# Reordering the opening's up blocks and computing more up blocks of the second feed-forward by seven products

## The chip, the cores and the metric

The kernel runs on one core of a Trainium2 chip, as one launch. The metric is the device time of one execution in microseconds (us). One core has five engines with instruction streams of their own: TensorE (PE in the profile; its weight loads are PEld), VectorE (DVE), ScalarE (ACT), GpSimd (POOL) and SyncE (SP), which issues most transfers. An engine runs its instructions in their order and waits for the others by semaphores. Sixteen DMA engines move data between HBM and the on-chip buffer. TensorE writes its sums into eight banks of PSUM, each 128 x 512 numbers of four bytes.

## The reference, cut to what matters

One layer with a context and a latent sequence of 256 tokens each and a model width of 2048. Each half-step feed-forward has 5632 hidden channels.

```python
def adaln(x, g, mod, i):
    return rms_norm(x, g) * (1 + mod[:, i + 1, None, :]) + mod[:, i, None, :]

def half_step_ffn(x, mod, i, g, w_up, w_down):
    h = adaln(x, g, mod, i)
    a, b = jnp.split(h @ w_up, 2, axis=-1)
    return x + 0.5 * mod[:, i + 2, None, :] * ((jax.nn.silu(a) * b) @ w_down)

mod_l = (silu(c) @ w_mod + b_mod).reshape(B, 9, D_MODEL)        # mod_c likewise from c_ctx
xl = half_step_ffn(xl, mod_l, 0, g_norm[0], w_ffn1_up, w_ffn1_down)
xc = half_step_ffn(xc, mod_c, 0, g_norm[0], w_ffn1_up, w_ffn1_down)
...                                                             # token mixing of both sequences
xl = half_step_ffn(xl, mod_l, 6, g_norm[2], w_ffn2_up, w_ffn2_down)
return rms_norm(xl, g_final)
```

So the first feed-forward works on 512 tokens, the second on the 256 latent ones alone.

## The kernel before, in words

**Numbers in two parts.** Every matrix operand of 32 bits is held as a high part (rounded to the format that TensorE multiplies) and a low part (the rest). `split` (line 110) makes both from a raw weight tile of 128 x 2048, in two halves of 128 x 1024: ScalarE copies the high part (line 118), VectorE subtracts it (line 119). `hi` and `lo` have four buffers each, `raw` three. `mm3` (line 138) makes one product from three matmuls: high x high (140), high x low and low x high (141 and 142). `load_split` (line 131) loads a tile on SP's queue and splits it, and takes one step of whatever is in `beside["load"]`.

**The hidden channels** come in 44 columns of 128; four columns make a block, so there are eleven blocks (0 to 10). A column f has an a and a b half, each of which sums 16 rows of weights k = 0 to 15 (2048 inputs).

**The opening** (lines 459 to 612). The scale and shift of the first feed-forward's norm aren't known at the start: they come from 32 units of 1 MB of modulation weights. The loop over `BLOCKS` (line 577: row blocks 0, 1, 2-4, 4-6 ... 14-16) loads a row block's units, sums them on TensorE (`mod_sums`, line 541; output `tr<-mraw,cP`), and, for one unit of each two-row block, on VectorE against the conditions `cB`. It turns the sums, scales the transposed x into the operands `hhi` and `hlo` for these rows, and then adds these rows' products to the columns f = 0, 1, 2 (`products`, line 413), which hold all six `mm` banks of PSUM until the end. The columns of one row block run between the sums of the next. Ahead of the loop stands the preparation: x and ctx are loaded, `spread` (line 483) lays the two condition vectors over all partitions by matmuls against ones (`mm<-raw,ones`), first the context's, then the latents'; `x_tile` squares, sums and scales each of four x tiles; `x_turned` transposes row 0. Instructions of this stage are pinned to the program's order (most carry line 78).

After the loop, `tail` (line 664) takes silu(a) x b of columns 0 to 2, and column f = 3 is computed by itself from four more tiles (lines 680 to 688).

**Seven products.** Blocks 1 to 10 of the first feed-forward's up part (`quad`, line 761) cut tokens and inputs in two each, and combine seven products of half size instead of eight; the operands for that (`n1`, `s2`, `s4`, `s3`) are sums and differences of token quarters that `token_forms` (line 698) makes on VectorE and ScalarE ahead of and during the first such block. The weight combinations arise in two chain buffers by accumulating transfers on POOL's queue (`accum`, issued at line 652).

**The second feed-forward** (from line 1780). Blocks 1, 3, 5, 7 and 9 are computed by seven products (`quad`, line 1920: 7 products x 2 tiles, 12 matmuls a tile), blocks 2, 4, 6, 8 and 10 plainly (`up`, line 2000: 8 tiles, 24 matmuls a tile). A `down` (line 2034) multiplies a finished hidden block by four tiles of the down weights, 24 matmuls each, and adds the sums into `acc2`. `units` strings up and down tiles together; after each unit the loop at the end of the stage takes tiles of the seven-product blocks at `PACE2` = 70/73 per unit, so the two kinds alternate nearly one to one. `turned` transposes a finished hidden tile. In a seven-product block of this stage (the list `order`) the two chain buffers receive three pairs of accumulating loads and the two `ra` tiles one pair; `plain`, `loaded` and `again` are plain loads. `mod_late` adds one modulation sum on VectorE (line 211, `sraw`) in some of the loads, paced by ((32, 62),). Then come `down` of block 9 and `last2`, the last block with the final norm.

Of the kernel before, what the change touches and what calls it, by code (L numbers as in the profile page):

```python
# [19 lines left out]
P = 128  # L20
D = 2048
# [12 lines left out]
PACE2 = 70 / 73  # L34

BLOCKS = ((0, 1), (1, 2)) + tuple((k, k + 2) for k in range(2, 16, 2))
# [13 lines left out]
def tile_layer(ctx: ExitStack, tc: tile.TileContext, I: dict, out: bass.AP):  # L50
# [59 lines left out]
    def split(raw, n=2048):  # L110

        half = n // 2
        parts = []
        for h in range(2):
            hi = wp.tile([P, 1024], F32R, tag="hi", name="hi", bufs=4)[:, :half]
            lo = wp.tile([P, 1024], F32R, tag="lo", name="lo", bufs=4)[:, :half]
            src = raw[:, h * half : (h + 1) * half]
            nc.scalar.activation(hi, src, AF.Copy)  # L118
            vector[0].tensor_tensor(lo, src, hi.bitcast(F32), op=ALU.subtract)  # L119
# [339 lines left out]
    pre = [[bank(), bank()] for _ in range(NPRE)]  # L459
    with pool(name="st", bufs=1) as st:  # L460
        scratch.append(st)
        cP = st.tile([P, KT, 32], F32, name="cP")
# [20 lines left out]
        def spread(s, m):  # L483
            for q in range(4):
                b = pre[q // 2][q % 2]
                w = slice(q * CB, (q + 1) * CB)
                tensor[0].matmul(b, ones[:32, :], m[:, w], start=True, stop=True)
                if s:
                    nc.scalar.activation(cB[:, s, w], b, AF.Copy)
                else:  # L490
                    vector[0].tensor_copy(cB[:, s, w], b)

        def x_tile(s, t, shared=False):
# [3 lines left out]
            for cb in range(NCB):  # L497
                if not (shared and cb % 2):
# [5 lines left out]
            for c in (slice(0, 256), slice(256, D)):  # L504
                vector[0].tensor_scalar(x[:, c], x[:, c], r, None, op0=ALU.mult)

# [12 lines left out]
        tc.keep_in_program_order(nc.sync.dma_start(vecs, I["vecs"]))  # L519
        diagonals = [diagonal(s) for s in (CTX, LAT)]  # L520
        spread(CTX, diagonals[0])
        x_tile(CTX, 0)
        x_turned(0, CTX, 0)
        spread(LAT, diagonals[1])
        for s, t in ((CTX, 1), (LAT, 0), (LAT, 1)):
            x_tile(s, t, s == LAT and t == 1)
            x_turned(0, s, t)
# [7 lines left out]

        def mod_unit():
            raw = st.tile([P, 2048], F32, tag="mraw", name="mraw", bufs=4)
# [38 lines left out]
        turns = []  # L576
        for k0, k1 in BLOCKS:
            kk = slice(k0, k1)
            following = products(I["w_up1"], pre, k0, k1, hhi, hlo, k0 == 0)
            if k1 - k0 == 2:  # L580
                raw = mod_unit()
            for i in range(2):
                for _ in mod_sums(i, k0 if i else k1 - 1, k1, following if i else iter(())):
                    steps(prods, 3 - (k1 - k0))
                if k0 == 0:
                    mod_turned()
# [6 lines left out]
            mod_turned()  # L593
            steps(prods)
            for s in (CTX, LAT):
                scale_of(0, s, kk)
            if k1 - k0 == 1:
# [5 lines left out]
                x_scaled(k0, tb)  # L603
            else:
# [6 lines left out]
        drain(prods)  # L611
        vector[0], tensor[0] = nc.vector, nc.tensor
# [40 lines left out]
    with pool(name="f1u", bufs=1) as f1u:  # L653
# [10 lines left out]
        def tail(f, pab):  # L664
            sa = ca_tile()
            nc.scalar.activation(sa, pab[0], AF.Silu)
            nc.vector.tensor_tensor(sa, sa, pab[1], op=ALU.mult)
            nc.sync.dma_start(hidd[0][:, :, f, :], sa.rearrange("p (t c) -> p t c", t=4))

# [8 lines left out]
        for f in range(NPRE):  # L678
            tail(f, pre[f])
        for f in range(NPRE, FB):  # L680
            pab = []
            for ab in range(2):
                wt = load_split(I["w_up1"][f, ab])
                b = bank()
                for k in range(KT):
                    mm3(b, *wt(slice(k * P, (k + 1) * P)), hhi[:, k, :], hlo[:, k, :], k == 0, k == KT - 1)
                pab.append(b)
            tail(f, pab)
# [68 lines left out]

        def c12_tile():
            return f1u.tile([P, CB], F32, tag="c12", name="c12", bufs=2)
# [89 lines left out]
        def first_steps(step):  # L849
            if step in (1, 2, 3, 4, 5, 6):  # L850
# [21 lines left out]
        raws, place0 = [], []  # L872
        quad(1, first_steps)
# [900 lines left out]
    with f2x:  # L1774
# [53 lines left out]
        beside["load"] = mod_late(f8cm.__enter__(), 8, 9, ((32, 62),))  # L1828
# [3 lines left out]
        QUADS = range(1, LAST, 2)  # L1832
# [16 lines left out]
        def token_forms():  # L1849
# [20 lines left out]
            v = ra_tile()[:, :1024].rearrange("p (k c) -> p k c", k=8)  # L1870
# [9 lines left out]
            v = ra_tile()[:, :1024].rearrange("p (k c) -> p k c", k=8)  # L1880
            difference(v, a11, a21)
            put(s3, v)
# [3 lines left out]
        turn = []  # L1886
        summed = set()

        def turned():

            if not turn:
                return
            n, t, sa, sign = turn[0]
# [19 lines left out]
        def wait_turn(n, t, sa, sign):  # L1913
            turn.append((n, t, sa, sign))
# [5 lines left out]
        def quad(n):  # L1920
# [41 lines left out]
            def again(q):  # L1962
                if n + 2 in QUADS:
                    nc.sync.dma_start(chain_[q], part(n + 2, 0, q))

            def loaded(q):
                ra[q] = ra_tile()
                nc.sync.dma_start(ra[q], part(n, 1, 2 + q))
                return ra[q]

            def plain(q):
# [262 lines left out]
```

## Time and profile before

| what | value |
|---|---|
| median of 3 runs | 2656.78 us (2656.41 to 2657.49) |
| the profiled execution | 2654.22 us, its span 2652.5 us |
| granted TensorE clock, mean | 0.998 |
| bytes read from HBM / written | 659.87 MB / 17.89 MB |
| plain transfers (q1) / POOL's (q0) | 500.07 MB / 177.22 MB |
| modulation units of the opening | 32 of 1024 KB, 7.5 us from issue to landing in the median |

In a table of windows each row is a stretch of the span: its ends and length, the busy time and number of instructions of each engine, the granted clock, the mean busy share of the DMA engines and their GB/s. In a timeline a row has a start, a duration, the engine, the line, the instruction, output <- inputs, the shapes and the count; in brackets how long the engine was idle before it and what released it. In a table of groups the last numbers are the busy time, the mean duration in ns, and the idle time of the engine before them. Line 78 is the helper that pins the opening's order.

### The profile page before, as it was taken

How to read it: one execution, taken by the hardware profiler on the slowest of the kernel's cores; microseconds unless marked ns; L12 is line 12 of the kernel's file. 1: busy time of each engine (PE TensorE's matmuls, PEld its weight loads, DVE VectorE, ACT ScalarE, POOL GpSimd, SP SyncE). 2: the span in 40 equal slices, each digit the busy share in tenths (PEclk: the TensorE clock that was granted, in tenths of full speed). 3: DMA queues.
4: the chain of work that ended last, by engine and by line, in shares of the span. 5: the costliest groups of instructions: out<-in, count | busy, mean ns of one | idle time of the engine just before them, and what ended most of it. 6: DMA issues, size and time to landing. Idle time of an engine off the chain costs nothing. (4 is left out here: it accounts for less than half of the span.)

```text
span 2652.5 us, 33763 instructions
## 1 busy us (share of the span) xinstructions
PE 2603.8 (98%) x12718; PEld 2153.9 (81%) x12718; DVE 2132.9 (80%) x2918; ACT 1349.5 (51%) x1682; POOL 208.3 (8%) x259
## 2 busy tenths in 40 slices
PE   8999999999999999999999999999999999999998
PEld 4688887888888878888889888877898888888887
DVE  5697888878888788888886979797698777777877
ACT  4354444554444555444455336355476655555554
POOL 0000001000001100010110000111000000000001
PEclk9999999999999999999999999999999999999999
DMA  9979999999999988889986867574479998989975
GB/s 360 340 214 270 264 278 262 263 276 281 261 283 263 274 233 239 223 208 229 231 243 224 308 232 242 199 270 167 167 262 291 288 291 291 288 275 283 276 231 175
DMA packets 135028, 679.98 MB, mean 256 GB/s; under 512 B 14152, under 2 KB 23624, under 8 KB 73552
## 3 DMA queue, kind: packets, MB, share of 16 engines
q1 hardware_dynamic: 107216, 500.07, 50.8%
q0 software_dynamic: 27360, 177.22, 34.2%
q8 instruction: 100, 1.64, 0.2%
q10 hardware_dynamic: 288, 0.52, 0.1%
q14 instruction: 64, 0.52, 0.1%
HBM read 659.87 MB, written 17.89 MB: 256 GB/s over the span
## 5 line engine op out<-in xcount | busy, mean ns | idle before, releaser
L118 ACT ACTIVATE hi<-raw 128x1024 fp32r<-128x1024 f32 (+3 forms) x542 | 560.8, 1039 | 639.1 <-PE mm L142 481.8
L119 DVE TENSOR_TENSOR lo<-raw,hi 128x1024 fp32r<-128x1024 f32 (+1 forms) x524 | 631.1, 1211 | 272.2 <-ACT hi L118 254.9
L118 ACT ACTIVATE hi<-chain 128x1024 fp32r<-128x1024 f32 x320 | 337.9, 1059 | 257.6 <-PE mm L142 135.7
L119 DVE TENSOR_TENSOR lo<-chain,hi 128x1024 fp32r<-128x1024 f32 x320 | 387.5, 1221 | 95.8 <-ACT hi L118 93.1
L140 PE MATMUL mm<-hi,hhi 128*128 128x512 f32 (+3 forms) x1024 | 390.7, 384 | 7.3 <-DVE c L755 6.8
L141 PE MATMUL mm<-lo,hhi 128*128 128x512 f32 (+3 forms) x1024 | 387.6, 379 | 0.2
L142 PE MATMUL mm<-hi,hlo 128*128 128x512 f32 (+3 forms) x1024 | 387.0, 378 | 0.0
L211 DVE SCALAR_TENSOR_TENSOR junk<-sraw,cBh 128x1024 fp8e5<-128x1024 f32 x192 | 234.4, 1221 | 24.8 <-DMA sraw<-in_w_mt 22.5
L140 PEld LDWEIGHTS mm<-hi,hhi 128*128 128x128 f32 x1024 | 192.3, 188 | 40.0 <-ACT hi L118 6.4
L142 PEld LDWEIGHTS mm<-hi,hlo 128*128 128x128 f32 x1024 | 192.5, 188 | 33.6
L141 PEld LDWEIGHTS mm<-lo,hhi 128*128 128x128 f32 x1024 | 192.7, 188 | 32.0 <-DVE lo L119 1.3
L142 PE MATMUL mm<-hi,hid2l 128*128 128x512 f32 x352 | 137.4, 390 | 0.0
L140 PE MATMUL mm<-hi,hid2h 128*128 128x512 f32 x352 | 137.2, 390 | 0.0
L141 PE MATMUL mm<-lo,hid2h 128*128 128x512 f32 x352 | 137.1, 389 | 0.0
L140 PE MATMUL mm<-hi,h2hi 128*128 128x512 f32 x320 | 125.0, 391 | 1.5 <-DVE sab L1813 1.5
L141 PE MATMUL mm<-lo,h2hi 128*128 128x512 f32 x320 | 124.6, 389 | 0.0
L142 PE MATMUL mm<-hi,h2lo 128*128 128x512 f32 x320 | 124.6, 389 | 0.0
L652 POOL DMA_DIRECT2D chain<-in_w_up1b x60 | 53.1, 886 | 739.4 <-DVE lo L119 654.4
L142 PE MATMUL mm<-hhi,lo 128*128 128x512 f32 (+1 forms) x288 | 100.4, 349 | 4.5 <-DVE lo L119 4.4
L140 PE MATMUL mm<-hhi,hi 128*128 128x512 f32 (+1 forms) x288 | 101.3, 352 | 0.0
L141 PE MATMUL mm<-hlo,hi 128*128 128x512 f32 (+1 forms) x288 | 99.4, 345 | 0.0
L211 DVE SCALAR_TENSOR_TENSOR sr<-sr,cBl 128x1024 f32<-128x1024 f32 x72 | 87.1, 1216 | 7.0 <-DMA sr<-in_w_mt 6.8
(479 smaller groups left out, 5483.8 us busy)
## 6 DMA issues: line engine op xcount, KB each, us to landing
raw<-in_w_dn SPq DMA_DIRECT2D x70, 1024.0 KB, 7.3
sraw<-in_w_mt SPq DMA_DIRECT2D x128, 512.0 KB, 7.5
chain<-in_w_up1b POOLq DMA_DIRECT2D x60, 1024.0 KB, 11.1
raw<-in_w_up2b SPq DMA_DIRECT2D x50, 1024.0 KB, 7.0
raw<-in_w_up1b SPq DMA_DIRECT2D x40, 1024.0 KB, 8.5
sr<-in_w_mt SPq DMA_DIRECT2D x69, 512.0 KB, 5.3
mraw<-in_w_m SPq DMA_DIRECT2D x32, 1024.0 KB, 7.5
chain<-in_w_dn POOLq DMA_DIRECT2D x30, 1024.0 KB, 8.8
```

Of the source, the lines that this page charges most:

```text
L118: nc.scalar.activation(hi, src, AF.Copy)
L119: vector[0].tensor_tensor(lo, src, hi.bitcast(F32), op=ALU.subtract)
L140: tensor[0].matmul(out_ap, sh, mh, start=first, stop=False, skip_group_check=skip)
L141: tensor[0].matmul(out_ap, sh, ml, start=False, stop=False, skip_group_check=skip)
L142: tensor[0].matmul(out_ap, sl, mh, start=False, stop=last, skip_group_check=skip)
L211: ins = nc.vector.scalar_tensor_tensor(junk() if junk else raw, raw, 1.0, cB[s], op0=ALU.mult, op1=ALU.mult, accum_out=mT[:, i, s, kt, h : ...
L652: accum = lambda dst, src: nc.gpsimd.dma_start(dst, src, accum_op=ALU.add)
```

## The change

In the opening, the three columns that a row block serves take turns: 0, 1, 2 for rows 0 to 4, then 1, 2, 3 to row 10, then 2, 3, 0. What a column lacks is done later: f = 3's rows 0 to 4 from the row block that begins at 6, f = 0's rows 4 to 10 from the one that begins at 12 (`LATER`), f = 1's rows 10 to 16 inside the first seven-product block (`back`). When column 0 or 1 gives up its two banks, its sums so far go to HBM (`put_by`) and are added back later by an accumulating load (`whole_sums`). The products of a load run in three passes over all its columns: the weights' high parts with the high parts of the activations, then with their low parts, then the weights' low parts. The preparation is woven: only the context's half of the spread stands first, the latents' four matmuls follow one by one, two of them behind the modulation sums of row 0; only 256 of the 2048 columns of each x tile are scaled at once, the rest during row blocks 0 and 2; the sums of squares are shared between ScalarE and VectorE.

The buffers of `split` become one ring of four slots for `hi` and one for `lo`. In the second feed-forward a whole tile is split at once (`split_whole`, two slots), and its products are ordered so that all that need the high part come first. The plain blocks are 2, 6 and 9; the other seven are computed by seven products. One accumulating pair of each such block becomes a plain load, made earlier, with an addition on VectorE (`added`). The token forms use `acc2` as scratch. The order of the tiles is a table (`places`), and `turned` waits until three tiles' worth of work has been issued since the tile was ready. The pace of `mod_late` is ((32, 52),).

```diff
-PACE2 = 70 / 73
+COLUMN_PLAN = _column_plan()     # fs = (0, 1, 2) if k1 <= 4 else (1, 2, 3) if k1 <= 10 else (2, 3, 0)
+PUT_BY = {(0, 4): 3, (1, 10): 0}
+LATER = {6: [(3, 0, 4)], 12: [(0, 4, 8), (0, 8, 10)]}
...
+    def split_whole(raw):
+        hi, lo = ring(2)
+        nc.scalar.activation(hi, raw, AF.Copy)
+        nc.vector.tensor_tensor(lo, raw, hi.bitcast(F32), op=ALU.subtract)
+        return lambda w: (hi[:, w], lo[:, w])
+    def high_first(*parts):
+        for out_ap, sh, sl, mh, ml, first, last in parts:
+            nc.tensor.matmul(out_ap, sh, mh, start=first, stop=False, skip_group_check=True)
+            nc.tensor.matmul(out_ap, sl, mh, start=False, stop=False, skip_group_check=True)
+    def low_last(*parts):
+        for out_ap, sh, sl, mh, ml, first, last in parts:
+            nc.tensor.matmul(out_ap, sh, ml, start=False, stop=last, skip_group_check=True)
...
+                for wl, tl in ((0, 0), (0, 1), (1, 0)):
+                    for o, (f, ab, k) in enumerate(each):
...
+                        tensor[0].matmul(slot[f][ab], wt(slice(o * P, o * P + P))[wl], (hhi, hlo)[tl][:, k, :], start=first, stop=bool(last))
...
+                        if done % (3 if g[0][2] - g[0][1] == 1 else 6) == 0:
+                            yield
...
+                            nc.scalar.activation(t, slot[f][ab], AF.Copy)
+                            nc.gpsimd.dma_start(put_by[f][ab], t)
...
+        def opening(following):
...
+            for n, (s, t) in enumerate(xs0):
+                scaled = x_sums(s, t, 2 if n else 3)
+                wide[n](vector[0].tensor_copy)
+                scaled(slice(0, 256))
+                rest.append(lambda scaled=scaled: scaled(slice(256, D)))
+                if n == 3:
+                    drain(mod_sums(0, 0, 1))
+                x_turned(0, s, t)
+                for q in {1: (0,), 2: (1,)}.get(n, ()):
+                    late(q)
+            mod_turned()
+            drain(mod_sums(1, 0, 1))
+            steps(following)
+            mod_turned()
+            for q in (2, 3):
+                late(q)
...
+            if k0 in LATER:
+                back = columns([[x] for x in LATER[k0]])
+                steps(back)
...
         def first_steps(step):
+            if step == 0:
+                steps(back)
+            if step in (1, 2, 3):
+                steps(back, 2)
+            if step == 4:
+                drain(back)
+                tail(0, *first_of[0], first_of[0][0])
+                first_of[1] = whole_sums(1)
+            if step == 7:
+                tail(1, *first_of[1], first_of[1][0])
...
+        back = columns([[(1, 10, 14)], [(1, 14, 16)]])
         quad(1, first_steps)
...
-        QUADS = range(1, LAST, 2)
+        PLAIN = (2, 6, 9)
+        QUADS = [n for n in range(1, LAST + 1) if n not in PLAIN]
...
+            def added(q):
+                nc.vector.tensor_tensor(chain_[q], chain_[q], ra[q], op=ALU.add)
...
-                (a12, plain, "Y", True, None, c11),
-                (n1, held, "Y", True, chained(1, 2), kept),
-                (s4, loaded, "Y", False, lambda q: accum(ra[q], part(n, 1, q)), p35),
+                (a12, plain, "Y", True, loaded, c11),
+                (n1, held, "Y", True, lambda q: added(0) if q else None, kept),
+                (s4, lambda q: ra[q], "Y", False, lambda q: (None if q else added(1), accum(ra[q], part(n, 1, q))), p35),
...
+            halves = iter((4, 0, 4, 0, 0, 4, 0, 0, 4, 0, 4, 0, 0, 4, 0))
...
+            for n in QUADS:
+                last = n == QUADS[-1]
+                for i in range(14):
+                    out.append(i in (range(3, 10) if last else (3, 4, 5, 6, 7, 9, 11, 13)) or n == QUADS[-2] and i == 8)
```

More of the change, by code (lines that the diff above doesn't have):

```diff
@@ L481, in diagonal, with spread, x_sums @@
             return m
[L483 to L493, printed above, removed]
+        def spread(s, m, q, b):
+            w = slice(q * CB, (q + 1) * CB)
+            tensor[0].matmul(b, ones[:32, :], m[:, w], start=True, stop=True)
+            return lambda copy: copy(cB[:, s, w], b)
+        def x_sums(s, t, n_act):
             x = xs0[s, t]
@@ L497, in x_tile @@
             for cb in range(NCB):
-                if not (shared and cb % 2):
+                if cb < n_act:
                     sumsq(ss4[:, cb : cb + 1], x[:, cb * CB : (cb + 1) * CB])
@@ L593, in tile_layer @@
             mod_turned()
+            while k0 == 2 and rest:
+                rest.pop(0)()
             steps(prods)
@@ L603, in tile_layer @@
                 x_scaled(k0, tb)
+                if not k0:
+                    rest.pop(0)()
+                    rest.pop(0)()
             else:
@@ L677, in tile_layer, with c12_tile @@
             first_chain(1, c)
[L678 to L688, printed above, removed]
+        def c12_tile():
+            return f1u.tile([P, CB], F32, tag="c12", name="c12", bufs=2)
+        for f in (2, 3):
+            tail(f, *slot[f], ca_tile())
+        first_of = {0: whole_sums(0)}
         n1, s2, s4 = form("n", "n1"), form("s", "s2"), form("t", "s4")
```

223 lines of the change are left out of this document (160 added, 63 removed).

## The prediction, as it was put on record before the change was timed

> **What bounds the kernel now.** I read the first part of the page, then the stages as windows, then TensorE in order of time inside the two stages that the change touches, and last the groups and transfers there.
>
> ```profile
> span 2652.5 us, 33763 instructions
> PE 2603.8 (98%) x12718; PEld 2153.9 (81%) x12718; DVE 2132.9 (80%) x2918; ACT 1349.5 (51%) x1682; POOL 208.3 (8%) x259
> ```
>
> ```profile
> core 0: us, PE busy (x) PEld busy (x) DVE busy (x) ACT busy (x) POOL busy (x), PEclk, DMA share, GB/s
> 0.00:22.18 22.18, 15.00 (x19) 5.34 (x19) 13.21 (x21) 13.90 (x34) 3.95 (x21) 1.00 0.91 362
> 22.18:31.24 9.06, 6.31 (x104) 4.24 (x104) 4.48 (x12) 4.03 (x10) 0.06 (x2) 1.00 0.93 344
> 31.24:61.05 29.81, 27.01 (x240) 17.27 (x239) 18.07 (x38) 8.97 (x18) 0.00 (x0) 0.94 0.94 355
> 61.05:116.85 55.80, 53.70 (x445) 36.83 (x444) 38.77 (x68) 20.36 (x40) 0.00 (x0) 1.00 0.98 363
> 116.85:144.08 27.23, 25.76 (x169) 19.03 (x167) 20.92 (x31) 12.22 (x22) 0.00 (x0) 1.00 0.70 269
> 144.08:165.90 21.82, 21.82 (x98) 18.08 (x97) 21.82 (x20) 10.31 (x12) 1.04 (x1) 1.00 0.83 244
> 165.90:240.60 74.70, 74.70 (x335) 61.88 (x334) 60.32 (x65) 37.72 (x42) 6.29 (x8) 1.00 0.88 235
> 1985.69:2576.00 590.31, 590.31 (x2636) 488.21 (x2637) 451.64 (x473) 338.26 (x354) 34.98 (x40) 1.00 0.91 281
> ```
>
> The rows are: the opening up to the end of the spread products, to the first columns, to the third block of two rows, four such blocks, the last ones; then the fourth column (f = 3) alone; the first seven-product block; the second feed-forward from its first plain up block to the end of its last seven-product block. From 144.08 us on TensorE never waits in these rows. There, time is the number of matmuls times their pitch. In the opening it is idle for 7.18 + 2.75 + 2.80 + 2.10 + 1.47 = 16.3 us, while the transfers run at a share of 0.91 to 0.98.
>
> A duration is no pitch, since matmuls overlap. Three rows give the pitch:
>
> ```profile
> 2551.89 0.39 PE L140 MATMUL mm<-hi,h2hi 128*128 128x512 f32 x1
> 2557.33 0.39 PE L140 MATMUL X<-hi,s3f 128*128 128x512 f32 x1
> 2560.05 0.39 PE L140 MATMUL mm<-hi,h2hi 128*128 128x512 f32 x1
> ```
>
> From the first to the second lie the 24 matmuls of one tile of a plain block, 5.44 us; to the third the 12 of one tile of a seven-product block, 2.72 us. Both give 0.2267 us each.
>
> **The second feed-forward.** A plain up block has 2 halves (a and b) x 4 tiles x 4 rows of weights x 2 token blocks x 3 = 192 matmuls; a seven-product one 7 products x 2 tiles x 4 x 3 = 168. Five of each become three and seven: 2 x 24 = 48 matmuls fewer, 48 x 0.2267 = 10.9 us. All of it lies on the engine that never waits, so the whole sum counts if the others keep up. What they get:
>
> ```profile
> L119 DVE TENSOR_TENSOR lo<-chain,hi 128x1024 fp32r<-128x1024 f32 x80 | 96.1, 1220 | 5.6 <-ACT hi L118 4.3
> L2046 DVE TENSOR_TENSOR acc<-acc,mm 128x512 f32<-128x512 f32 x71 | 48.4, 681 | 1.8 <-PE mm L142 1.8
> L211 DVE SCALAR_TENSOR_TENSOR sraw<-sraw,cBl 128x1024 f32<-128x1024 f32 x32 | 39.0, 1218 | 0.0
> L1922 DVE TENSOR_TENSOR ca<-Y,ca 128x512 f32<-128x512 f32 x10 | 6.8, 684 | 0.0
> L2109 DVE TENSOR_TENSOR lo<-raw,hi 128x2048 fp32r<-128x2048 f32 x2 | 4.6, 2284 | 0.0
> ```
>
> VectorE: each of the two changed blocks has 6 more tiles to split at 2.28 (the whole-tile row, L2109) and 4 more short ops at 0.68: 2 x 16.4 = 33 us. The new `added` is two adds of 128x2048 in each of seven blocks; the trace has no such add, so I take the subtraction of that shape, 2.28: 14 x 2.28 = 32 us. Whole tiles instead of halves save at most 2 x 1.22 - 2.28 = 0.16 us on some 150 tiles, 24 us, at least nothing where halves already follow one another. From 451.6 this makes 493 to 517 us of 579: 85 to 89%, against 77% now. It stays beside TensorE's work, with little room. One turn of a seven-product block holds 14 x 2.72 + 8 x 5.44 = 81.6 us of matmuls. VectorE has 16 x 2.28 (splits and adds), 8 x 0.68 (ends and hidden tiles), 8 units x 3.2 (a split and, over all units, 0.9 of sums), and five modulation sums at 1.3: 74 us. So 8 us stay free per turn. Within it tiles 0 to 2 run with no plain unit beside them; there VectorE has 2.28 of every 2.72 us bound to splits. The order of products (both that need the high part first, 8 of 12, then the 4 that need the low part) lets a low part come 1.8 us late (8 x 0.2267). ScalarE gains 12 tiles at 2 x 1.06 us (the row below), 25 us on 338, and stays under two thirds.
>
> ```profile
> L118 ACT ACTIVATE hi<-chain 128x1024 fp32r<-128x1024 f32 x320 | 337.9, 1059 | 257.6 <-PE mm L142 135.7
> ```
>
> Transfers in this stage:
>
> ```profile
> chain<-in_w_up2b POOLq DMA_DIRECT2D x28, 1024.0 KB, 10.7
> ra<-in_w_up2b POOLq DMA_DIRECT2D x10, 1024.0 KB, 10.8
> chain<-in_w_up2b SPq DMA_DIRECT2D x8, 1024.0 KB, 7.0
> ```
>
> A block issued 8 accumulating loads on POOL's queue and 6 on SP's; now 6 and 6, since `loaded` moves one step earlier and `added` does on VectorE what the second accumulating pair did. In all 42 instead of 40 accumulating loads, 66 instead of 70 plain ones (7 x 6 + 3 x 8 against 5 x 6 + 5 x 8): about the same traffic, at a share of 0.91 now. `added` is a new wait: on the load of `ra`, issued three tiles and two units ahead (some 19 us against 7.0). Behind it on VectorE stand the next low parts, for which TensorE waits after 1.8 us. The next block's first tile is loaded by `again` two tiles and one unit ahead, 10.9 us against 7.0: the thinnest cover. After the last block its end (add, silu, multiply, three ops of about 0.68) stands before the transposes of its hidden tile with less work behind it than now. I take 3 us of waiting for all of that; bounds 0, and 16 us if one add of each block were uncovered (7 x 2.28). Net: -10.9 + 3 = **-7.9 us**.
>
> **The opening.** Nothing is removed from it. The loop now holds three columns per row block as before (288 matmuls), plus f = 3's rows 0 to 4 (24) and f = 0's rows 4 to 10 (36); f = 1's rows 10 to 16 (36) go into the first seven-product block; the separate 96 of f = 3 (the row 144.08:165.90) go. So 13.6 us move forward and 8.2 back, and the gain is the idle time that they and the new order fill. Its rows:
>
> ```profile
> 5.59 7.19 PE L78 MATMUL mm<-raw,ones 32*128 32x512 f32 x8 [2.47 <-DVE raw L78]
> 29.60 0.50 PE L78 MATMUL mm<-hhi,hi 128*128 128x512 f32 x1 [1.15 <-ACT hhi L392]
> 32.59 1.94 PE L78 MATMUL tr<-mraw,cP 128*32 128x128 f32 x32
> 38.45 1.08 PE L78 MATMUL tr<-mraw,cP 128*32 128x128 f32 x32
> 56.81 1.07 PE L78 MATMUL tr<-mraw,cP 128*32 128x256 f32 x16 [0.77 <-DMA mraw<-in_w_m]
> 112.65 1.07 PE L78 MATMUL tr<-mraw,cP 128*32 128x256 f32 x16 [1.12 <-DMA mraw<-in_w_m]
> ```
>
> Half of the latents' spread and most of the scaling of x move behind the first row, so the modulation sum that now starts at 32.59 can start some 5 us earlier. But at 56.81 and 112.65 TensorE waits for modulation weights: up to there the loads, not the products, set the time, and what is won before 56.81 is mostly handed back. The loads can gain only their own gaps up to 116.85: 9% less the first 2.2 us, 7%, 6% and 2% of the rows above, about 3.5 us. Against it the shifted columns bring 1.3 MB more into the loop (60 matmuls use 20 weight tiles of 64 KB, three each), 3.6 us at 363 GB/s, though late, where products fill the wait. I take 4 us; bounds 0, and 10.8, all idle time behind the first product at 5.59.
>
> The Trainium skill ("DMA: Bandwidth & Descriptors", Where 436 GB/s comes from) puts loads from HBM at about 358 GB/s per core. The row 61.05:116.85 has 363, so the measured one stands. By that rule the added 1.3 MB costs 3.7 us and nothing can speed the loads up, which speaks against this part of the change: that is rival B, and the trace bears it out as far as its two waits go.
>
> The first seven-product block pays. VectorE is full while f = 3 runs (21.82 of 21.82), making the token forms; then it has 60.32 of 74.70. Without f = 3 the same work (82.1 less f = 3's remaining splits, plus f = 1's splits and tails, about even) must fit into 74.7 + 8.2 = 82.9 us. It is at its limit. I take 2 us of waiting; bounds 0 and 8 (a tenth of the stretch). Net for the opening: -4 + 2 = **-2 us**, bounds -10.8 and +8.
>
> TensorE's clock: 0.94 in 31.24:61.05, 1.8 us lost, and 1.94 against 1.08 us for the same 32 products. I leave it as it is. The Trainium skill ("TensorE: Matmul & The Clock Gate", Part 1) has the clock at half after an idle window of about 3.4 us; the new order has shorter waits there, and by that rule the sum would be 1.8 us lower, within the range. No trace here shows which.
>
> **The sum**: -7.9 - 2 = -9.9 us. The profiled execution took 2654.22 (span 2652.5 and 1.7 around it): 2644.3. The median of the runs shown lies 2.56 higher; so **2647 us**.
>
> **Rivals.**
> A. Everything is fed: -10.9 in the feed-forward, -8 in the opening, no wait in the first block: 2638. For it: 23% of VectorE is free now. Against: the full row at 144.08. 0.15.
> B. Loads bind the opening and the first block waits for VectorE: opening +2, feed-forward -7.9: 2651. For it: the waits at 56.81 and 112.65. 0.17.
> C. The feed-forward's low parts come late in the runs without plain units, 1.2 us in each of seven turns beside the 3 above: 8.4 us more than the forecast, 2655. For it: 0.44 us of VectorE per tile there. Against: the high parts come first. 0.08.
> D. Slower: VectorE becomes the bound of the second feed-forward, at `added`. If both adds of each block stand in front of a low part that is due, 14 x 2.28 = 32 us: 2657 - 10.9 - 2 + 32 = 2676; with one of them 2660. It decides from the point where VectorE loses over 8 us per turn to ops that stand waiting, its margin above. Against: 8 units per turn give it places to catch up. 0.07.
> E. The change doesn't do what it says: the shared ring makes a split wait for slots that are still in use, in every stage, and eats the saving: 2656. Against: as many slots (four of 1024) as before. 0.03.
> The forecast keeps 0.50.
>
> **The numbers.** A change under 0.2% (5.3 us) can't be told from none. Faster by that (under 2651.5): the forecast, A and most of B, 0.78; within: the rest of B, C and E, 0.14; slower: D and a tail of C, 0.08. The range 2638 to 2656 takes in A to C.
>
> **What would show it.** In the changed profile: groups X and Y 7/5 as many, the plain group 3/5 (192 of each third); TensorE's windows full from the first plain block on, VectorE near 87%; no wait for a low part beyond 3 us in sum; f = 3's own row gone, the first seven-product block starting near 152 us; TensorE idle some 4 us less before it. Wrong would be: TensorE waiting for `lo` or `chain` every turn, or the first block later than 158 us, which is 165.9 less the 8.2 moved into it.

## The result and the profile after

The changed kernel takes 2671.51 us (median; 2669.55 to 2674.11) against 2656.6 us before: ratio 1.0057, 95% interval 1.0045 to 1.0069. A second measurement gave 1.0059 (1.0040 to 1.0078). The prediction was 2647 us, so it has the wrong sign: 15 us lost instead of 10 won.

First the page of the changed kernel, its span and busy times:

```profile
span 2668.7 us, 33372 instructions
...
PE 2603.0 (98%) x12670; PEld 2149.6 (81%) x12670; DVE 2183.4 (82%) x2813; ACT 1346.9 (50%) x1551; POOL 214.3 (8%) x269
```

TensorE has 48 matmuls fewer (12718 before) and is busy as long as before (2603.8). The work was saved and the time was not, so some of it ran at a lower clock or stood waiting. To place the loss, take an event that both kernels have after the first seven-product block: the like transposes in the second one. Timeline of before, then of after (start, duration):

```profile
301.41 0.60 PE L750 MATMUL tr<-ident,ca 128*128 128x128 f32 x4
```

```profile
321.41 0.60 PE L886 MATMUL tr<-ident,ca 128*128 128x128 f32 x4
```

After 321 us the changed kernel is 20.0 us late; its span ends 2668.7 - 2652.5 = 16.2 us late. So the opening and its first block lost 20.0 us, and the second feed-forward won 3.8 (the 1684.2 us between the two, from this event to the first plain up block of the second feed-forward, are the same in both). Since the first block ended at 240.60 before, it ends at 240.60 + 20.00 = 260.60 now. The stages as windows of the changed kernel, cut like those of the prediction:

```profile
core 0: us, PE busy (x) PEld busy (x) DVE busy (x) ACT busy (x) POOL busy (x), PEclk, DMA share, GB/s
0.00:31.24 31.24, 25.38 (x133) 11.65 (x137) 18.40 (x41) 14.44 (x34) 4.00 (x21) 1.00 0.93 371
31.24:61.05 29.81, 25.39 (x248) 17.40 (x241) 20.61 (x41) 11.61 (x23) 0.00 (x0) 1.00 0.97 359
61.05:116.85 55.80, 54.56 (x437) 39.01 (x435) 40.23 (x64) 20.68 (x41) 2.39 (x4) 1.00 0.91 345
116.85:157.34 40.49, 37.26 (x223) 28.09 (x223) 20.61 (x35) 11.53 (x22) 0.00 (x0) 0.92 0.47 183
157.34:260.60 103.26, 90.17 (x370) 71.13 (x370) 80.63 (x85) 48.54 (x58) 10.55 (x12) 0.93 0.90 246
2005.65:2597.00 591.35, 586.83 (x2610) 484.06 (x2611) 496.85 (x366) 332.73 (x228) 37.10 (x42) 1.00 0.89 276
```

The last row is not the same work as before's last row, because the order of the tiles changed; from the first plain up block to the end of the span it is 663.0 us, against 666.8 before.

The opening up to the first block ends at 157.34, against 165.90 less the 8.2 us of matmuls that moved into the block: 0.4 us won. The block itself takes 103.26 us. Before it took 74.70, with the moved matmuls 82.9: 20.4 us lost, of which 13.1 are TensorE's idle time (103.26 - 90.17) and the rest, some 7 us, its clock of 0.93. VectorE is busy for 80.6 of the 103 us, so no engine is full. TensorE's waits there, in order of time (the bracket has the idle time before the instruction and what ended it); the first line is the opening's:

```profile
120.08 1.94 PE L89 MATMUL tr<-mraw,cP 128*32 128x256 f32 x16 [4.47 <-DMA mraw<-in_w_m]
...
162.39 0.50 PE L192 MATMUL mm<-ringlo,hhi 128*128 128x512 f32 x1 [4.20 <-DVE ringlo L170]
...
199.17 0.50 PE L191 MATMUL mm<-ringhi,n1h 128*128 128x512 f32 x1 [1.82 <-ACT ringhi L169]
200.43 0.56 PE L192 MATMUL mm<-ringlo,n1h 128*128 128x512 f32 x1 [0.76 <-DVE ringlo L170]
...
233.78 0.80 PE L191 MATMUL mm<-ringhi,s2h 128*128 128x512 f32 x1 [4.47 <-ACT ringhi L169]
```

Behind each stands a queue kept in order. At 120.08 it is SP's:

```profile
101.83 0.33 SPq L637 DMA_DIRECT2D mraw<-in_w_m  x1
102.21 0.42 SPq L744 DMA_DIRECT2D ccd<-cc  x1
110.49 1.41 SPq L530 DMA_DIRECT2D raw<-in_w_up  x3
112.40 4.04 SPq L637 DMA_DIRECT2D mraw<-in_w_m  x4
```

The loads of the next columns wait until 110.49 for a raw tile (three exist, and the columns done later hold them too); the modulation's loads stand behind. At 162.39 it is VectorE's, where ops of the token forms run ahead of the low part that TensorE needs:

```profile
158.85 1.22 DVE L835 TENSOR_TENSOR sraw<-sraw,hlo 128x1024 f32<-128x1024 f32 x1
159.98 1.22 DVE L835 TENSOR_TENSOR n1l<-sraw,n1h 128x1024 fp32r<-128x1024 f32 x1
161.12 1.22 DVE L170 TENSOR_TENSOR ringlo<-chain,ringhi 128x1024 fp32r<-128x1024 f32 x1
```

At 199.17 and at 233.78 it is ScalarE's. Timeline of ScalarE, then two groups of transfers (count, size, time to landing):

```profile
197.54 0.63 ACT L800 ACTIVATE c<-c 128x512 f32<-128x512 f32 x1 [4.10 <-DMA c<-by]
...
232.18 0.60 ACT L913 ACTIVATE c<-mm 128x512 f32<-128x512 f32 x1 [9.94 <-DMA hid<-c]
```

```profile
hid<-ca SPq DMA_DIRECT2D x2, 256.0 KB, 5.3
...
hid<-c SPq DMA_DIRECT2D x1, 256.0 KB, 27.1
```

ScalarE first stands behind the accumulating load that brings back f = 1's put-by sums, then behind a store: the copy of Y takes a c12 tile from which f = 1's block of hid is still leaving, 27.1 us after its issue. The splits due next stand behind both.

In the second feed-forward two groups waited (us in sum, times, longest), and the clock fell once:

```profile
PE tr L2045 <- DVE ca L2067: 4.5, 5, 1.4
PE mm L153 <- DVE sab L1957: 1.9, 1, 1.9
```

```profile
2006.00:2010.00 4.00, 4.00 (x12) 3.15 (x11) 3.87 (x4) 0.74 (x2) 0.00 (x0) 0.57 0.87 342
```

No low part and no `added` is among them.

### The profile page after: what moved, and what is told of

Read it like the earlier page. It is cut to its first block, busy times and chain, and to the rows that moved or that the text cites. A ratio compares the mean times of both kernels' runs of the same rounds, so it can differ in the third digit from the quotient of the medians.

```text
span 2668.7 us, 33372 instructions
## 1 busy us (share of the span) xinstructions
PE 2603.0 (98%) x12670; PEld 2149.6 (81%) x12670; DVE 2183.4 (82%) x2813; ACT 1346.9 (50%) x1551; POOL 214.3 (8%) x269
## 5 line engine op out<-in xcount | busy, mean ns | idle before, releaser
L169 ACT ACTIVATE ringhi<-raw 128x1024 fp32r<-128x1024 f32 (+4 forms) x363 | 370.8, 1025 | 444.1 <-PE mm L193 291.2
L170 DVE TENSOR_TENSOR ringlo<-raw,ringhi 128x1024 fp32r<-128x1024 f32 (+3 forms) x342 | 408.9, 1203 | 140.5 <-ACT ringhi L169 124.4
L191 PE MATMUL mm<-ringhi,hhi 128*128 128x512 f32 (+3 forms) x1024 | 391.8, 385 | 6.5 <-DVE c L891 5.9
L192 PE MATMUL mm<-ringlo,hhi 128*128 128x512 f32 (+3 forms) x1024 | 388.1, 379 | 4.5 <-DVE ringlo L170 4.4
L193 PE MATMUL mm<-ringhi,hlo 128*128 128x512 f32 (+3 forms) x1024 | 387.7, 379 | 0.0
L170 DVE TENSOR_TENSOR ringlo<-chain,ringhi 128x1024 fp32r<-128x1024 f32 x240 | 291.3, 1222 | 96.4 <-ACT ringhi L169 95.0
L169 ACT ACTIVATE ringhi<-chain 128x1024 fp32r<-128x1024 f32 x240 | 253.0, 1059 | 230.7 <-PE mm L193 116.6
L191 PEld LDWEIGHTS mm<-ringhi,hhi 128*128 128x128 f32 x1024 | 192.7, 188 | 39.6 <-ACT ringhi L169 6.9
L192 PEld LDWEIGHTS mm<-ringlo,hhi 128*128 128x128 f32 x1024 | 193.0, 188 | 37.5 <-DVE ringlo L170 6.8
L193 PEld LDWEIGHTS mm<-ringhi,hlo 128*128 128x128 f32 x1024 | 192.9, 188 | 33.5
L139 ACT ACTIVATE ringhi<-chain 128x2048 fp32r<-128x2048 f32 x56 | 107.4, 1918 | 78.5 <-PE mm L154 23.4
## 6 DMA issues: line engine op xcount, KB each, us to landing
chain<-in_w_up1b POOLq DMA_DIRECT2D x60, 1024.0 KB, 10.8
```

The lines of the kernel that those rows point to most:

```text
L139: nc.scalar.activation(hi, raw, AF.Copy)
L191: tensor[0].matmul(out_ap, sh, mh, start=first, stop=False, skip_group_check=skip)
L192: tensor[0].matmul(out_ap, sh, ml, start=False, stop=False, skip_group_check=skip)
L193: tensor[0].matmul(out_ap, sl, mh, start=False, stop=last, skip_group_check=skip)
```

## The experiments

The ratio is to the kernel before, measured on the same chip. "Transposes" is the time of the event above in the profiled execution (301.41 before). One opening scatters: the first block began at 155.3 to 161.5 us in six profiles of kernels that issue the same work up to there, or nearly so. The opening that by_early and open_mended share puts the transposes at 296.00 and at 300.51. So single profiles are compared by their waits, kernels by their ratio.

| kernel | ratio (95% interval) | transposes, us |
|---|---|---|
| open_only | 1.0087 (1.0066 to 1.0109) | 323.62 |
| ff2_only | 0.9982 (0.9972 to 0.9992) | 302.92 |
| own_store | 1.0079 (1.0060 to 1.0098) | 326.64 |
| forms_late | 1.0080 (1.0063 to 1.0097) | 327.12 |
| drain_first | 1.0076 (1.0052 to 1.0100) | 320.32 |
| later_pool | 1.0114 (1.0099 to 1.0129) | 333.65 |
| drain_later | 1.0103 (1.0087 to 1.0119) | 339.65 |
| ff2_delay6 | 0.9971 (0.9960 to 0.9983) | 302.60 |
| after_again | 1.0059 (1.0040 to 1.0078) | 321.11 |
| unit_first | 1.0030 (1.0018 to 1.0042) | 317.28 |
| tails_late | 1.0033 (1.0021 to 1.0044) | 315.65 |
| mended | 0.9995 (0.9986 to 1.0005) | 309.32 |
| by_only | 1.0064 (1.0049 to 1.0079) | 321.75 |
| by_early | 0.9958 (0.9945 to 0.9971) | 296.00 |
| all_in_block | 0.9964 (0.9949 to 0.9980) | 301.93 |
| open_mended | 0.9984 (0.9975 to 0.9993) | 300.51 |

**Which half loses.** Two kernels take the diff apart: open_only has its parts up to the end of the first seven-product block, ff2_only those of the second feed-forward (both with the ring).

> The opening part alone: up blocks in turns and the rows left to the first seven-product block, with the second feed-forward as before. Theory 1 (the loss is made before 260 us: at quad 2's like transposes the changed kernel stands 20.0 us behind): 20 us slower than before, about 2676.6. Theory 2 (the loss is in the second feed-forward, by VectorE): within 3 us of before. If parts disturb each other, the two parts alone do not add up to the 14.9 us of the whole change.

> The second feed-forward's part alone: seven of ten up blocks by seven products, whole-tile splits, high before low, with the opening as before. Theory 1: 3.8 us faster than before (666.8 us from its first up block to the end of the span before, 663.05 after), about 2652.8. Theory 2: 10 us or more slower. The prediction's own term for this part was 7.9 us faster, 2648.7.

The opening's part loses 0.87%, some 23 us, and the other half wins 0.18%, 4.8 us (2.1 to 7.4). Multiplied they give 1.0069, at the edge of the whole's interval: nothing shows that the halves disturb each other, and theory 2 falls.

**One wait at a time.** own_store lets the product go to a tile of its own:

```diff
-nc.vector.tensor_tensor(sa, sa, b, op=ALU.mult)
+nc.vector.tensor_tensor(out, sa, b, op=ALU.mult)     # out: stg for f = 1
```

> The changed kernel, with the product that leaves as f=1's block of hid written to stg, which is free then, instead of onto a c12 tile, so that the copy of Y to that c12 tile no longer waits for the store. If the 27.1 us landing of that store costs what TensorE lost at 228 to 240 (23 matmuls in 12 us, which take 5.2 us at the steady pitch): 6.8 us faster than the changed kernel, 2664.7. Rival: the accumulating loads that share the queues with the store (DMA share 0.97 to 1.09 from 204 to 232) bind next: under 2 us faster.

forms_late moves the token forms behind the splits:

```diff
-        steps(forms, 2)
...
-            if step in (1, 2, 3, 4, 5, 6):
+            if step < 7:
                 steps(forms)
```

> The changed kernel, with the two steps of the token forms that ran ahead of the first seven-product block moved behind its first splits, one step of the forms at each of its steps 0 to 6. If VectorE's form operations ahead of the chain tile's low part are what TensorE waits for at 162.39 (4.20 us, and half clock after it): 4 to 6 us faster than the changed kernel, about 2666.5. Rival: VectorE's work in that block is the same and falls due later, so the wait moves to n1's products at step 4: within 1.5 us.

by_only fetches the put-by sums early by plain loads and adds them on VectorE (and has by_early as its counterpart further on):

```diff
-                nc.scalar.activation(x, b, AF.Copy)
-                accum(x, before)
+                nc.sync.dma_start(x, before)          # ahead of the block
...
+                nc.vector.tensor_tensor(x, b, x, op=ALU.add)
```

> The changed kernel with that one edit (the rows stay in the block, the store from the c12 tile too). ScalarE's 4.1 us on the accumulating load at 197 goes, and with it TensorE's 1.71 and 0.76 us and the half clock behind them (200 to 204): 3 to 5 us faster than the changed kernel, ratio 1.004. The store that is 27 us in flight still holds the c12 tile, so TensorE's 4.5 us near 232 stay. Rival: without that wait the later ones grow: 1.005 to 1.006.

None of the three gained; each ratio lies at or above the changed kernel's. In each the wait aimed at is gone and another has grown. TensorE and VectorE in own_store, where no copy waits for the store any more:

```profile
243.54 0.76 PE L191 MATMUL mm<-ringhi,hhi 128*128 128x512 f32 x1 [4.61 <-DVE c L892]
```

```profile
241.56 1.23 DVE L262 SCALAR_TENSOR_TENSOR junk<-sraw,cBh 128x1024 fp8e5<-128x1024 f32 x1 [5.71 <-DMA sraw<-in_w_mt]
```

VectorE stood in order behind a modulation load, with the add that frees TensorE's bank behind it. In forms_late the first wait shrank to 0.17 us, and the left rows' own split came late:

```profile
176.37 3.78 PE L556 MATMUL tr<-hhi,ringhi 128*128 128x512 f32 x8 [5.90 <-ACT ringhi L169]
```

In by_only the first wait and the one behind the store grew:

```profile
162.82 0.79 PE L192 MATMUL mm<-ringlo,hhi 128*128 128x512 f32 x1 [6.62 <-DVE ringlo L170]
...
233.34 0.80 PE L191 MATMUL mm<-ringhi,s2h 128*128 128x512 f32 x1 [6.73 <-ACT ringhi L169]
```

**The left rows ahead of the block, and another queue for the up loads.** drain_first multiplies f = 1's rows 10 to 16 ahead of the block and closes f = 0 and f = 1 at once; later_pool issues the late up loads on GpSimd's queue; drain_later does both.

```diff
...
+        drain(back)                                   # drain_first
+        first_of[1] = whole_sums(1)
+        for f in (0, 1):
+            tail(f, *first_of[f], first_of[f][0])
...
-pin(nc.sync.dma_start(raw[:, o : o + w]...            # later_pool
+pin(queue.dma_start(raw[:, o : o + w]...              # nc.gpsimd for these
```

> The changed kernel, with the rows of f=1 that were left to the first seven-product block multiplied ahead of it, and both open blocks of hid finished there, so that the block itself is as before (the up columns in turns and the second feed-forward stay changed). Theory 1a (the left rows and what hangs on them, beside the forms and the chain, cost the block 20 us; the 36 matmuls alone are 8.2 us wherever they stand): 15 to 20 us faster than the changed kernel, near the kernel before (ratio 0.998 to 1.002). Rival 1b (the block is slow because it starts while forms, splits and loads are due at once, whoever fills its start): under 8 us faster, ratio above 1.004.

> The changed kernel, with the up loads of the last blocks (10, 12, 14) and of the columns done later issued by GpSimd's queue, so that a load that waits for a raw slot does not stand ahead of the modulation's loads on SP. If that is what TensorE waits for near 120 us (4.3 to 4.5 us in five profiles, then a clock of 0.83 to 0.86): the first seven-product block starts 6 to 8 us earlier, the kernel is 6 us faster than the changed kernel. Rival 1: the raw slots themselves are late, so the wait moves to the up columns: under 2 us. Rival 2: the block that follows is bound by VectorE and the loads and eats the gain: it starts earlier and ends no earlier.

> Both edits, rows multiplied ahead of the first seven-product block and the late up loads on GpSimd's queue. If the two losses are separate: the sum of the two gains, near 2649 (ratio 0.996 to 0.999). If one hides the other: no better than drain_first.

All three missed. drain_first asks ScalarE for the closing product right behind the accumulating load; ScalarE, and TensorE a little later:

```profile
186.92 0.63 ACT L800 ACTIVATE c<-c 128x512 f32<-128x512 f32 x1 [10.25 <-DMA c<-by]
```

```profile
191.34 0.79 PE L192 MATMUL mm<-ringlo,hhi 128*128 128x512 f32 x1 [8.75 <-DVE ringlo L170]
```

So it only moved a wait, and says nothing against 1a or for 1b. In later_pool the wait for the modulation's load is gone, but an up load now stands on GpSimd's queue behind the store of the put-by sums, which waits for ScalarE (44.17 us of idle queue), and TensorE waits for that load:

```profile
61.45 1.33 POOL L568 DMA_DIRECT2D by<-by  x2 [44.17 <-ACT by L567]
62.75 0.76 POOL L531 DMA_DIRECT2D raw<-in_w_up  x1
```

```profile
73.61 2.93 PE L89 MATMUL mm<-hhi,ringhi 128*128 128x512 f32 x6 [10.10 <-ACT ringhi L169]
```

drain_later has such a wait twice, 9.82 us before 77.19 and 9.52 us before 133.54.

**The second feed-forward's transposes.**

```diff
-            if not turn or turn[0][-1] + 3 > tiles[0]:
+            if not turn or turn[0][-1] + (6 if turn[0][1] else 3) > tiles[0]:
```

> ff2_only (the second feed-forward's part alone, opening as before), with the second half's transposes of each seven-product block kept back six tiles of work in place of three. If TensorE's 4.0 to 4.5 us on those transposes (4 or 5 waits for VectorE's last product of the block, behind the next block's chain split) are what is left of the loss there: 4 us faster than ff2_only, ratio to before 0.9967. Rival: what hangs on the transposes (the down products and the next block's tiles) comes late in turn: as ff2_only, 0.998.

0.9971, 7.7 us (4.5 to 10.6) below before; the intervals of ff2_only and this one overlap, the traces do not: the waits on the transposes are gone, and little has come in their place (all waits of ff2_delay6 from 1970 us on, 2.6 us in sum).

```profile
PE mm L153 <- ACT ringhi L139: 1.1, 1, 1.1
PE X L159 <- DVE ringlo L140: 0.9, 2, 0.7
PE mm L153 <- DVE sab L1864: 0.6, 1, 0.6
```

**The opening's two losses by better edits.** after_again is the changed kernel, beside the others. unit_first swaps two lines for the blocks from row 10 on; tails_late is drain_first with the closing products at steps 2 and 5, the second into stg, the load of the left rows first and the forms behind the splits; mended is both with ff2_delay6's edit.

```diff
-                if g == KT // nk - 1:
+                if g == KT // nk - 1 and k0 < 10:
                     steps(last)
                 raw = mod_unit()
+                if g == KT // nk - 1 and k0 >= 10:
+                    steps(last)
```

> The changed kernel as it is, beside the others of this group: its ratio to the kernel before was 1.0057 in its first measurement, and kernels that differ from it only inside or behind the first seven-product block came out at 1.008. If the opening's start scatters from run to run (the first seven-product block began at 157.3 to 161.5 us in five profiles of one and the same opening): 1.005 to 1.008.

> The changed kernel, with the last modulation load of the blocks from row 10 on issued on SP ahead of the next columns' load instead of behind it. Theory: that load stands behind an up load that waits for a raw slot (SP's columns' load at 110.49, the modulation's at 112.40, TensorE's wait at 120.08); it goes, and with it the half clock: the first seven-product block starts 6 us earlier, 4 to 6 us faster than after_again. Rival: the next wait (the columns' own load, now later) takes its place: within 2 us. Second rival: the block starts earlier and its own waits grow by as much.

> The changed kernel, with the rows left of f=1 multiplied ahead of the first seven-product block as in drain_first, but both closing products at steps 2 and 5 of that block (so that neither ScalarE nor VectorE stands behind the accumulating load of the put-by sums, 15.6 us in drain_first), the second one's result in stg, and the token forms behind the splits. Theory: the block's loss is a queue of in-order waits, each on a load or store that is 10 to 27 us in flight; with all of them moved off, the block takes the 75 to 80 us that it takes before: 12 to 20 us faster than after_again, ratio 0.999 to 1.002. Rival: the loads themselves are too late at the block's start (DMA share 1.0 at 160 to 180), so a wait on a load takes the place: under 6 us faster.

> unit_first and tails_late together with the transposes of the second feed-forward kept back six tiles. If the opening's two losses are what was found and are separate: ratio 0.994 to 0.998, below ff2_delay6 (0.9971) if the opening's part then gains at all. If the opening's part gains nothing even so: 0.998 or above, and the best is the second feed-forward's part alone.

unit_first won 0.29%, 7.7 us, by swapping the order of two issues: no wait near 120 us is left, and TensorE is busy at full clock up to the block, which begins at 150.94:

```profile
116.85:150.94 34.09, 34.09 (x217) 26.22 (x207) 20.69 (x36) 11.62 (x22) 0.00 (x0) 1.00 0.52 203
```

tails_late won 7 us, short of the 12 to 20 expected. The gains add up: 1.0059 less 0.0029, 0.0026 and ff2_delay6's 0.0011 is 0.9993, and mended measured 0.9995, outside the 0.994 to 0.998 that was expected: the opening's part still gained nothing. What mended still loses in the block, ScalarE first:

```profile
174.58 0.63 ACT L803 ACTIVATE c<-c 128x512 f32<-128x512 f32 x1 [7.74 <-DMA c<-by]
```

```profile
176.21 0.80 PE L191 MATMUL mm<-ringhi,hhi 128*128 128x512 f32 x1 [4.55 <-ACT ringhi L169]
```

**Without the accumulating load.** by_early is mended with by_only's edit.

> mended, with the put-by sums fetched back by plain loads on SP before the first seven-product block (issued behind the chain's two tiles) and added to the finished sums by VectorE, in place of ScalarE's copy and an accumulating load. Theory: what mended still loses in that block (TensorE's 4.55 us at 176.21 and 0.46 behind it, 2.6 and 0.8 us of clock at 160 to 200, 3.17 us and 1.8 us of clock near 221; the block's start is 5.3 us earlier than before's) comes from ScalarE and VectorE, which stand in order behind the accumulating loads (7.74 and 5.91 us): 6 to 8 us faster than mended, ratio 0.9965 to 0.9975, so the opening's part then costs nothing or gains 1 us. Rival: the block's own plain loads and the token forms are late by themselves: within 2 us of mended, 0.9988 to 1.0.

0.9958, 0.37% or 9.8 us below mended, a little more than expected: the theory holds, and the rival falls. The edit is the one of by_only, which took nothing off the changed kernel (1.0064 against 1.0057 and 1.0059) and takes 9.8 us off mended, where the other waits are gone. From its profile, the last stretch of the opening and the block, where 2.0 us of idle time and no drop of the clock are left:

```profile
116.85:156.79 39.94, 39.94 (x236) 31.43 (x234) 28.73 (x45) 17.26 (x28) 0.91 (x1) 1.00 0.66 249
156.79:235.19 78.40, 76.44 (x340) 62.70 (x339) 71.68 (x77) 41.30 (x47) 6.09 (x7) 1.00 0.98 264
```

**Sum of the waits, or place of the rows.** all_in_block has all the single edits, with the left rows still inside the block and the second feed-forward as in the changed kernel; their load is issued ahead of the chain's:

```diff
+        back = columns([[(1, 10, 14)], [(1, 14, 16)]])
+        steps(back)
         for c in range(2):
             first_chain(1, c)
```

open_mended is by_early's opening with the second feed-forward of before.

> The changed kernel with all the single edits at once (unit_first, own_store, forms_late, by_only, and the load of f=1's left rows issued ahead of the chain's), but with the left rows still multiplied inside the first seven-product block, and the second feed-forward as in the changed kernel. If the block's loss is that several engines stand in order behind transfers, so that taking away one wait uncovers the next and only all together count: 12 us or more faster than the changed kernel, ratio 1.001 or less. If the rows inside the block are themselves too much for VectorE there (80.6 us of the block's 103.3 in the changed kernel): not more than unit_first alone, 1.003.

> by_early's opening with the second feed-forward as before. By the like transposes (296.00 us in by_early, 301.41 before) the mended opening alone gains 5.4 us: ratio 0.998. If it gains nothing, by_early's 0.9958 is the second feed-forward's alone.

all_in_block measures 0.9964, and takes 0.95%, 25 us, off the changed kernel, by five edits: three that gained nothing alone, unit_first with its 7.7, and the load's place, which was not tried alone (drain_first has it too, and did not gain). The block with the rows inside (six of their 36 products run just ahead of it):

```profile
155.40:241.12 85.72, 83.33 (x369) 68.02 (x368) 78.50 (x85) 44.41 (x51) 7.00 (x8) 1.00 0.99 279
```

VectorE does the same 78.5 us as in the changed kernel (80.6), in 85.7 us instead of 103.3; TensorE idles for 2.4 us and its clock never falls. The transfers run at 279 GB/s there, against 246, so their rate was not the limit either. So it is the sum of the waits, not the place of the rows and not VectorE's load; how much each of the four edits besides unit_first contributes is not shown. open_mended: the mended opening alone wins 0.16%, 4.2 us (1.9 to 6.6); times ff2_delay6's 0.9971 it gives 0.9955, and by_early measured 0.9958.

by_early, 2643.5 us, beats both kernels. all_in_block with ff2_delay6's edit was not tried.

## Why the prediction was wrong

**The pitch and the count** held: 48 matmuls fewer in the page, and the groups (group, count, busy, mean ns, idle):

```profile
L153 PE MATMUL mm<-ringhi,h2hi 128*128 128x512 f32 x192 | 75.9, 395 | 1.9 <-DVE sab L1957 1.9
...
L153 PE MATMUL Y<-ringhi,h2hi 128*128 128x512 f32 x112 | 43.8, 391 | 0.0
```

**The second feed-forward, -10.9 + 3 = -7.9 us**, measured -3.8 in the profile and -4.8 (-7.4 to -2.1) as ff2_only. The direction was right, the waits too small: 4.5 us on the transposes, which the prediction named ("less work behind it than now") and took into its 3 us, 0.4 more on sab than before's 1.5, and 0.43 x 4 = 1.7 us of clock behind that; 6.6 in sum. ff2_delay6 shows that 3 us are enough: it took the transposes' waits away and stands at -7.7 (-10.6 to -4.5). VectorE has 496.9 us of work there, the low end of the forecast's 493 to 517. `added` and the next chain's load cost TensorE nothing directly; but a late load holds ScalarE ahead of a block's last silu (3.06 us before 2107.35), VectorE then takes a split ahead of the product, and the transposes come late (0.85 us at 2112.25). Rivals C and D fell: no wait for a low part, none at `added`. E fell with them: the stages between, which use the ring too, take as long as before.

**The opening, -4 us**, came out at -0.4. By the windows, the new order won 4.1 us up to 31.24 (idle 5.9 instead of 9.9), and lost 2.5 us of idle time from there to the block (8.9 against 6.4) and 1.4 us of clock (0.92 in 40.5 us against 0.94 in 29.8). The prediction expected the waits for modulation weights to hand the gain back through the loads' rate. The 363 GB/s that it took as the loads' rate was no limit: the changed kernel moved 384 in 20:40 and 406 in 60:80, where the kernel before moved 356 and 372. Near 120 us the order was: SP issued nothing between 102.6 and 110.49, and the GB/s fell to 162 in 108:112. unit_first, which changes nothing but that order, wins 7.7 us. (The prediction's bound of 10.8 us, the idle time behind 5.59, comes to 11.0 by its rows; nothing hangs on it.)

**The first seven-product block, "I take 2 us of waiting; bounds 0 and 8"**: this step failed, by 18 us: the block lost 20.4. The prediction added up VectorE's work and found that it fits, at its limit; it does fit, as all_in_block shows with 2.4 us of idle time. What failed is that a sum of work stood for the waits. The step did not look at what each in-order engine has ahead of the split that TensorE needs next: token forms on VectorE (4.20 us of TensorE's time); on ScalarE an accumulating load that brings put-by sums back (4.10 us, then 1.82 and 0.76 on TensorE), and a store out of a c12 tile that the block takes again (9.94 us, then 4.47 on TensorE). The store and the put-by sums, 1 MB out and 1 MB back, were not in the sum at all; its 1.3 MB are up weights. The bound of 8 was a tenth of the stretch, with no wait in it. No rival had it either: B is the nearest, and puts the wait on VectorE's load, where it was not. Nor did the signs of being wrong catch it: the block began at 157.34, before the 158 that was named, and TensorE did not wait for `lo` or `chain` every turn of the second feed-forward.

That by_early stands 11.2 us below before (7.7 to 14.6), near the forecast's -9.9, does not make the forecast right: it took edits that the prediction did not see a need for.

**The clock** was left as it was. It rose from 0.94 to 1.00 in 31.24:61.05, the other reading that the prediction had given, and fell to 0.92 ahead of the block. In the block it cost some 7 us (0.07 of 103.26), a third of the loss: to each us of waiting came half a us of slow matmuls.

## What to carry to other kernels

When a change moves work into a stretch that is already busy, list every wait that it puts on each in-order queue (a load behind a load that waits for a tile, an activation behind a transfer, a tile taken again while a store still reads it), not only each engine's sum of work. Engines can all have room on average and still pass one stall round: then removing a single wait uncovers the next and measures as nothing, and only the edits together show that the idea was sound. And a transfer whose data has been ready for over 80 us, as the put-by sums were, is fetched early by a plain load, not asked for at the point of use.

## What the runs showed of the hardware that was not expected

The same store of 256 KB took 27.1 us in the changed kernel, 25.8 in own_store, and 8.6 in all_in_block and 7.8 in by_early. In the first two the chain's two accumulating loads of 1 MB were issued within 1.7 us of each other just ahead of it, with more in the 15 us after; in the last two the accumulating loads came 4 to 8 us apart. But the bunching alone does not make the store late: forms_late has the same pattern (208.00 and 209.73, the store at 212.23, two more by 222.08), and its store took 9.4 us. What does stays open.

The clock stood at 0.50 in 120:124 and in 232:236 of the changed kernel, behind the waits of 4.47 us. The wait of 1.9 us that ends at 2005.65 was followed by 0.57 for 4 us, and the waits of 1.82 and 0.76 us at 199.17 and 200.43 by 0.59 in 200:204, while before's 1.5 us at the place of the former and the 1.96 us at 210.59 in by_early left the clock at 1.00. The Trainium skill ("TensorE: Matmul & The Clock Gate", Part 1) has the clock at half after an idle window of about 3.4 us. The longer waits agree with that; those under 2 us are shorter than the rule asks, and what decides between the short ones stays open.
